# Statistics of the norms summed by TensorE, an opening with other DMA order, and ScalarE costs of the planner changed

## The chip, the cores and the metric

The kernel runs on one core of one Trainium2 chip. The metric is the device time of one execution in microseconds, the lower the better. TensorE (PE in the profile) multiplies, VectorE (DVE) and ScalarE (ACT) work element by element, GpSimd (POOL) computes a few powers, and SyncE (SP) issues most of the loads. Each engine works through its own instructions in the order in which the program wrote them.

## The reference, cut to what matters

Two layers act on 512 latent tokens and 256 context tokens of width 1024. Each layer is a modulated RMSNorm, one input projection, three parallel groups (a two-way mLSTM, a gated MLP over chunks, a convolution module), an output projection with a gated residual, then a second modulated RMSNorm, a SwiGLU of width 2816 and another gated residual. A last RMSNorm ends it. All of it is in float32.

```python
def rmsnorm(t, g):
    t32 = t.astype(jnp.float32)
    y = t32 * lax.rsqrt(jnp.mean(t32 * t32, axis=-1, keepdims=True) + EPS)
    return (y * g).astype(t.dtype)
...
px = (rmsnorm(x, norm1_g[l]) * (1.0 + sc1) + sh1) @ w_in[l] + b_in[l]
...
x = x + g1 * (y_x @ w_out[l])
x = x + g2 * swiglu(rmsnorm(x, norm2_g[l]) * (1.0 + sc2) + sh2, w_gu[l], w_down[l])
...
return rmsnorm(x, final_g)
```

The shifts `sh` and scales `sc` come from a product of the conditioning vectors with `w_mod`. The mean of the squares over the 1024 features of each token is the "statistic" of which this study speaks.

## The kernel before, in words

**Layout.** The residual stream `xT` lies with features on the partitions: 8 tiles (k = 0 to 7) of 128 features by 768 tokens. Tokens come in two groups, `GA` (the 512 latent ones) and `GB` (the 256 of the context); the second half of layer 1 splits the latent ones into `GX0` and `GX1` of 256 each. Every large product is done three times, with a high and a low part of each operand: high by high, high by low, low by high (lines 528, 529 and 530 in `tiles`). ACT makes the high part (a cast), DVE the low part (a subtraction): for weights `hi` and `lo` (lines 457 and 334, 374 and 376), for normalised activations the two halves of `HH` (lines 868 and 879). PE can start the second product of a step only when the low half of `HH` is there.

**A norm.** `square` has ACT square a tile of `xT` as soon as its residual is added, and DVE adds it to a running sum `acc` (line 781). With all 8 tiles in, `rstd_rows` has PE multiply each piece of 128 tokens of the sum with a column of 1/1024 (`stat`, line 831). DVE adds EPS (`ms`, line 837), POOL takes the power -0.5 (`rs`, line 264), PE spreads the result over the partitions (`rstdb`, line 846). Then for each k DVE makes the normalised tile `nt` (line 914), and ACT and DVE its two halves in `HH`. Only the last norm, `final`, leaves its last square out of the running sum: there PE multiplies the square tile too and accumulates in PSUM.

**The opening.** `start` clears constants, ACT's queue loads `cT` into `csil` (a tile with 32 columns per k, of which two are loaded), `ident`, and the small parameters `cv[0]`, then later `masks` and `cv[1]`; ACT applies SiLU to `csil` in place. SP's queue loads `xT` in four pieces of two k each, then the weights in the order that `ORDER` sets: quarters of `w_mod` (`modq`, products `modps` on PE at line 670, and `modT` at 687) between the first projection weights. `early_stats` squares all 768 tokens of each k on ACT (line 793), DVE adds them one after the other into one tile (line 800, seven additions), and PE makes the statistic of both groups from the sum (line 815, 6 instructions). A float32 matmul shows as two rows in the trace: 6 instructions are 12 passes.

**What sets the order.** Nothing is scheduled on the chip: while the program is built, a planner (`Plan`) runs all steps as coroutines. A step names an engine and an estimate of its duration, and the planner emits next what could start earliest by its estimates. So each estimate (`ACT(n)` is 95 + 0.833 n ns, `ACTP(n)` 190 + 0.833 n, `DVE2`, `STT`, `PE`, `MM` and so on) moves instructions on every engine, and on the chip each engine then keeps to that order. DMAs report on one of eight semaphores that are handed out in turn over all queues, in the order of emission. A DMA that is given a semaphore which is still in use waits on its queue until the earlier DMA has landed.

## Time and profile before

| | |
|---|---|
| median of 3 runs | 1536.78 us (1536.64 to 1539.75) |
| the profiled execution | 1534.92 us |
| its span, first to last instruction | 1533.1 us |
| granted TensorE clock, mean | 0.995 |
| PE busy | 1488.5 us |
| DVE busy | 1147.0 us |
| ACT busy | 686.0 us |
| POOL busy | 33.7 us |

The profiled execution takes 1.8 us more than its span and 1.86 us less than the median. A busy engine is one that has an instruction in flight. "Idle before" with a releaser is time in which the engine had nothing in flight, and what ended it.

### The profile page before, as it was taken

The page shows a single profiled execution, that of the slowest core. Times are in us where ns is not written, and L with a number is a line of the kernel's source. Part 1 is how long each engine was busy: PE and PEld are TensorE (multiplying, and loading weights), DVE is VectorE, ACT ScalarE, POOL GpSimd, SP SyncE. Part 2 cuts the span into 40 slices and gives each one's busy share as a digit, 9 for nine tenths or more (in the row PEclk, how much of TensorE's full clock was granted, in tenths as well). Part 3 has the DMA queues.
Part 4 walks back from the last instruction along what each step waited for, and adds up shares of the span by engine and source line. Part 5 has one row for each costly group of instructions (what it writes and reads, how often), then busy time and mean ns, then how long its engine had stood idle before and what let it go on. Part 6 is the DMA issues. An engine that isn't in the chain of part 4 may idle for free.

```text
span 1533.1 us, 26131 instructions
## 1 busy us (share of the span) xinstructions
PE 1488.5 (97%) x10212; PEld 1390.5 (91%) x10212; DVE 1147.0 (75%) x2430; ACT 686.0 (45%) x1428; POOL 33.7 (2%) x50
## 2 busy tenths in 40 slices
PE   5999999999999999999999999999999999999997
PEld 4887888888899999999999998778999999999997
DVE  5569988865898896777767773696767977877865
ACT  4332257644643343433333343416656554544534
POOL 0000010000000000000000000000100000000000
PEclk9999999999999999999999999999999999999999
DMA  9434244423143434343433332213332233333331
GB/s 327 171 125 133 69 140 146 128 83 120 60 138 104 145 97 151 97 124 124 128 120 124 111 98 76 76 60 102 103 111 70 83 103 105 104 97 100 105 98 64
DMA packets 73848, 173.25 MB, mean 113 GB/s; under 512 B 7564, under 2 KB 19964, under 8 KB 73724
## 3 DMA queue, kind: packets, MB, share of 16 engines
q1 hardware_dynamic: 70956, 170.16, 35.0%
q10 hardware_dynamic: 2768, 1.42, 0.3%
q8 instruction: 80, 1.31, 0.3%
q14 instruction: 44, 0.36, 0.1%
HBM read 169.34 MB, written 2.21 MB: 112 GB/s over the span
## 4 chain that ended last, share of the span: by engine, by line
PE 81%; DVE 11%; DMA 4%; ACT 2%; issue 2%; POOL 0%; SPq 0%; POOLq 0%; DVEq 0%; ACTq 0%
PE mm L528 14%; PE mm L529 14%; PE mm L530 14%; PE bA L1912 5%; PE bA L1913 5%; PE bA L1914 5%; PE bC L1912 2%; PE bC L1913 2%; PE bC L1914 2%; DVE lo L376 1%; DMA raw<-in_wgu 1%; DVE lo L334 1%; PE bB L1912 1%; PE vp L1325 1%; PE bB L1913 1%
## 5 line engine op out<-in xcount | busy, mean ns | idle before, releaser
L528 PE MATMUL mm<-HH,hi 128*128 128x256 f32 (+2 forms) x1040 | 349.3, 336 | 0.2 <-ACT HH L1624 0.2
L529 PE MATMUL mm<-HH,hi 128*128 128x256 f32 (+2 forms) x1040 | 337.5, 324 | 5.6 <-DVE HH L879 4.5
L530 PE MATMUL mm<-HH,lo 128*128 128x256 f32 (+2 forms) x1040 | 336.7, 324 | 0.6 <-DVE lo L334 0.6
L374 ACT CAST hi<-raw 128x512 fp32r<-128x512 f32 (+2 forms) x361 | 209.6, 599 | 240.2 <-PE mm L529 46.2
L376 DVE TENSOR_TENSOR lo<-raw,hi 128x512 fp32r<-128x512 f32 (+2 forms) x361 | 229.0, 659 | 28.6 <-ACT hi L374 25.5
L528 PEld LDWEIGHTS mm<-HH,hi 128*128 128x128 f32 x1040 | 196.5, 189 | 18.8 <-issue 6.4
L529 PEld LDWEIGHTS mm<-HH,hi 128*128 128x128 f32 x1040 | 196.8, 189 | 18.0 <-DVE HH L879 5.6
L530 PEld LDWEIGHTS mm<-HH,lo 128*128 128x128 f32 x1040 | 196.3, 189 | 15.8 <-DVE lo L334 0.8
L528 PE MATMUL mm<-ffn,hi 128*128 128x256 f32 (+1 forms) x544 | 167.4, 308 | 0.0
L529 PE MATMUL mm<-ffn,hi 128*128 128x256 f32 (+1 forms) x544 | 167.0, 307 | 0.0
L530 PE MATMUL mm<-ffn,lo 128*128 128x256 f32 (+1 forms) x544 | 166.7, 307 | 0.1
L2051 DVE SCALAR_TENSOR_TENSOR xT<-mm,modc,xT 128x256 f32<-128x256 f32 (+2 forms) x208 | 96.1, 480 | 77.7 <-PE mm L530 77.2
L457 ACT CAST hi<-raw 128x1024 fp32r<-128x1024 f32 (+4 forms) x92 | 87.8, 963 | 129.1 <-PE mm L529 61.5
L1913 PE MATMUL bA<-T,hi 128*128 128x384 f32 (+1 forms) x468 | 145.4, 311 | 0.0
L334 DVE TENSOR_TENSOR lo<-raw,hi 128x1024 fp32r<-128x1024 f32 (+4 forms) x92 | 102.2, 1119 | 54.1 <-ACT hi L457 49.6
L727 DVE SCALAR_TENSOR_TENSOR macc<-raw,csil,macc 128x512 f32<-128x512 f32 x168 | 122.3, 743 | 0.8
L420 DVE TENSOR_TENSOR raw<-raw 128x512 f32<-128x512 f32 x156 | 103.8, 686 | 23.6 <-DMA raw<-in_wgu 22.8
L1912 PE MATMUL bA<-HH,hi 128*128 128x256 f32 (+1 forms) x384 | 112.1, 292 | 0.5 <-ACT d L1986 0.5
L1914 PE MATMUL bA<-HH,lo 128*128 128x256 f32 (+1 forms) x384 | 111.9, 291 | 0.0
L528 PEld LDWEIGHTS mm<-ffn,hi 128*128 128x128 f32 x544 | 102.3, 188 | 0.8 <-issue 0.6
L530 PEld LDWEIGHTS mm<-ffn,lo 128*128 128x128 f32 x544 | 102.2, 188 | 0.4 <-DVE lo L376 0.4
L529 PEld LDWEIGHTS mm<-ffn,hi 128*128 128x128 f32 x544 | 102.3, 188 | 0.0
(273 smaller groups left out, 3016.5 us busy)
## 6 DMA issues: line engine op xcount, KB each, us to landing
raw<-in_wmod SPq DMA_DIRECT2D x96, 512.0 KB, 3.8
raw<-in_wgu SPq DMA_DIRECT2D x88, 512.0 KB, 3.6
raw<-in_wb SPq DMA_DIRECT2D x36, 512.0 KB, 3.6
pbt<-dr SPq DMA_DIRECT2D x40, 256.0 KB, 3.6
raw<-in_wd SPq DMA_DIRECT2D x40, 256.0 KB, 2.6
raw<-in_wout SPq DMA_DIRECT2D x16, 512.0 KB, 3.6
raw<-in_wd SPq DMA_DIRECT2D x16, 384.0 KB, 3.3
raw<-in_wd SPq DMA_DIRECT2D x16, 320.0 KB, 2.8
```

Of the source, the lines that this page charges most:

```text
L334: dve.tensor_tensor(lo, r, hi.bitcast(F32), ALU.subtract)
L374: act.copy(hi, x)
L376: dve.tensor_tensor(lo, x, hi.bitcast(F32), ALU.subtract)
L420: dve.tensor_tensor(o, x, y, op)
L528: pe.matmul(o, lhsT=hi[:, k, :], rhs=hh, start=(j == 0), stop=False)
L529: pe.matmul(o, lhsT=hi[:, k, :], rhs=hl, start=False, stop=False)
L530: pe.matmul(o, lhsT=lo[:, k, :], rhs=hh, start=False, stop=(j == nk - 1))
L727: dve.scalar_tensor_tensor(a[g], s[:, i, :], c, a[g], ALU.mult, ALU.add)
L1912: pe.matmul(o, lhsT=hi[:, k], rhs=rh, start=start and k == 0, stop=False, skip_group_check=True)
L1913: pe.matmul(o, lhsT=hi[:, k], rhs=rl, start=False, stop=False, skip_group_check=True)
L1914: pe.matmul(o, lhsT=lo[:, k], rhs=rh, start=False, stop=k == 3, skip_group_check=True)
L2051: dve.scalar_tensor_tensor(x, p[:, a - h["t0"]:b - h["t0"]], MODC[l][:, 5, d, g["g"]:g["g"] + 1], x, ALU.mult, ALU.add)
```

## The change

1. `early_square` and `early_stats`: DVE adds only the pairs of k 0 and 1, 2 and 3, 4 and 5 (three additions). PE multiplies each of the three pair sums, and the squares of k = 6 and of k = 7 as they are, with the column of 1/1024, all accumulated in PSUM: 5 times 6 instructions in place of 6.
2. `square`: in every norm, no longer in the last alone, the eighth square can go to PE by itself. DVE's eighth addition is left out, and PE has twice as many statistic instructions there. The condition is read when the eighth square is emitted and seven sums are done.
3. `start`: `cT` is loaded into a tile of its own, `cin`, contiguous on both sides, and SiLU writes from it into `csil`. `masks` and `cv[1]` move from ACT's queue to SP's, behind the first norm.
4. Seven activations are planned at `ACTP`, 95 ns more each, in place of `ACT`.

```diff
     def square(k, grp, then):
         n, t0 = grp["n"], grp["t0"]
-        if then is final and ACC.get(t0, (0, 0, 0))[2] == KD - 1:
+        if ACC.get(t0, (0, 0, 0))[2] == KD - 1:
             yield W(ACC[t0][1])
...
             ACC[t0].append(s)
-            yield from final(grp)
+            yield from then(grp)
             return
...
-        if k:
+        if k % 2 == 0 and k < 6:
+            odd[k + 1] = s
+            fire(ev("sq", k))
+            return
+        if k < 6:
             yield W(ev("sq", k - 1))
             yield DVE2(T)
-            dve.tensor_tensor(a[0], a[0], s, ALU.add)
+            dve.tensor_tensor(s, s, odd[k], ALU.add)
             release("slot")
-        fire(ev("sq", k))
+        if k > 1:
+            yield W(ev("st", k - 2 if k < 7 else 6))
+        for g, q in p:
+            for j in range(g["n"] // P):
+                yield MM(P)
+                pe.matmul(q[:, j:j + 1], lhsT=s[:, g["t0"] + j * P:g["t0"] + (j + 1) * P], rhs=onesD,
+                          start=(k == 1 and j == 0), stop=(k == KD - 1), skip_group_check=True)
...
     def norm_lo(tag, l, which, t, k, grp):
...
-        yield ACT(n)
+        yield ACTP(n)
         act.activation(h[:, 0, k, o:o + n], t, AF.Identity, bias=sh)
...
-        act.dma_start(out=csil[:, :, 0:2], in_=cT_d)
+        act.dma_start(out=cin, in_=cT_d)
...
-        act.activation(csil[:, :, 0:2], csil[:, :, 0:2], AF.Silu)
+        act.activation(csil[:, :, 0:2], cin, AF.Silu)
...
-        act.dma_start(out=masks, in_=mk_d)
-        act.dma_start(out=cv[1], in_=cv_d[1])
         spawn(early_stats(), 0.5)
+        yield W(ev("h", 0, 0, 0, KD - 1))
+        yield DMA(P * (256 + NCV) * 4)
+        sp.dma_start(out=masks, in_=mk_d)
+        sp.dma_start(out=cv[1], in_=cv_d[1])
```

The other `ACTP` edits are of the same form: `norm_copy`, and the evacuations of the conv gate, q, o and u columns.

What this does to the order is shown at three places. On SP's queue at the start, before (`DMAHW0` to `DMAHW7` are the eight semaphores, and "waits" is what the DMA waits for ahead of its issue):

```order
L308 DMA xT_69<-in_xT 128x1536 x3
L308 DMA xT_69<-in_xT 128x1536 [waits DMAHW0_49]
L328 DMA raw_112<-in_wmod 128x4x256 [waits DMAHW1_49]
L328 DMA raw_129<-in_wmod 128x4x256 [waits DMAHW2_49]
L328 DMA raw_135<-in_wb 128x1024 [waits DMAHW3_49]
```

The same place after:

```order
L309 DMA xT_69<-in_xT 128x1536 x4
L329 DMA raw_113<-in_wmod 128x4x256
L329 DMA raw_130<-in_wmod 128x4x256 [waits DMAHW0_49]
L329 DMA raw_136<-in_wb 128x1024 [waits DMAHW1_49]
L329 DMA raw_147<-in_wmod 128x4x256 [waits DMAHW2_49]
```

`DMAHW0` is that of the load of `cT` in both. Before, the fourth piece of `xT` waits for it; after, the second load of `w_mod` does, and four pieces of `xT` and one load of `w_mod` wait for nothing.

On PE at the start, before (`stat` is the statistic, `modps` and `modT` the modulation, `rstdb` the spread of the reciprocal root, `mm` the first projection):

```order
L670 MATMUL modps<-raw,csil 32x128 x16
L687 MATMUL modT<-sel_79,mq 128x4
L815 MATMUL stat<-onesD,sq 128x1 x6
L670 MATMUL modps<-raw,csil 32x128 x16
L846 MATMUL rstdb<-ident,rs 128x128 x2
L687 MATMUL modT<-sel_79,mq 128x4
L846 MATMUL rstdb<-ident,rs 128x128 x4
L670 MATMUL modps<-raw,csil 32x128 x8
L528 MATMUL mm<-HH,hi 128x256
```

And after:

```order
L810 MATMUL stat<-onesD,sq 128x1 x12
L671 MATMUL modps<-raw,csil 32x128 x8
L810 MATMUL stat<-onesD,sq 128x1 x6
L671 MATMUL modps<-raw,csil 32x128 x8
L810 MATMUL stat<-onesD,sq 128x1 x6
L688 MATMUL modT<-sel_80,mq 128x4
L810 MATMUL stat<-onesD,sq 128x1 x6
L671 MATMUL modps<-raw,csil 32x128 x16
L854 MATMUL rstdb<-ident,rs 128x128 x2
L688 MATMUL modT<-sel_80,mq 128x4
L854 MATMUL rstdb<-ident,rs 128x128 x4
L671 MATMUL modps<-raw,csil 32x128 x16
```

The statistic stands in five groups of 6 instructions, the first two ahead of all modulation and the others between its loads; one more load of modulation (8 instructions) stands ahead of the first `mm`.

On DVE where layer 1 begins, from the `ms` of GB on, before (`xT` is a residual addition, `lo` the low part of a weight, `kb` a small scaling, `HH` the low half of the normalised tile):

```order
L781 TENSOR_TENSOR acc<-acc,sq 128x512
L2051 SCALAR_TENSOR_TENSOR xT<-mm,modc_82,xT 128x384
L914 SCALAR_TENSOR_TENSOR nt<-xT,gs,rstdb 128x256
L334 TENSOR_TENSOR lo<-raw,hi 128x1024
L1689 TENSOR_SCALAR kb<-cv_81 128x4
L914 SCALAR_TENSOR_TENSOR nt<-xT,gs,rstdb 128x256
L781 TENSOR_TENSOR acc<-acc,sq 128x512
L2051 SCALAR_TENSOR_TENSOR xT<-mm,modc_82,xT 128x384
L334 TENSOR_TENSOR lo<-raw,hi 128x1024
L879 SCALAR_TENSOR_TENSOR HH<-nt,modc_83,HH 128x256
L914 SCALAR_TENSOR_TENSOR nt<-xT,gs,rstdb 128x256
L879 SCALAR_TENSOR_TENSOR HH<-nt,modc_83,HH 128x256
```

And after:

```order
L922 SCALAR_TENSOR_TENSOR nt<-xT,gs,rstdb 128x256
L2059 SCALAR_TENSOR_TENSOR xT<-mm,modc_83,xT 128x384
L922 SCALAR_TENSOR_TENSOR nt<-xT,gs,rstdb 128x256
L335 TENSOR_TENSOR lo<-raw,hi 128x1024
L1697 TENSOR_SCALAR kb<-cv_82 128x4
L922 SCALAR_TENSOR_TENSOR nt<-xT,gs,rstdb 128x256
L887 SCALAR_TENSOR_TENSOR HH<-nt,modc_84,HH 128x256
L2059 SCALAR_TENSOR_TENSOR xT<-mm,modc_83,xT 128x384
L335 TENSOR_TENSOR lo<-raw,hi 128x1024
L782 TENSOR_TENSOR acc<-acc,sq 128x512
L887 SCALAR_TENSOR_TENSOR HH<-nt,modc_84,HH 128x256
L922 SCALAR_TENSOR_TENSOR nt<-xT,gs,rstdb 128x256
```

The first `HH` of the context group has moved ahead of one `lo` and one `acc`; the second now stands behind an `xT`, a `lo` and an `acc` that follow the first. In the same stretch PE has `stat` with 4 instructions in place of 2 for GB; for GA it keeps 4, since there the eighth square is emitted before the seventh sum is done, so the condition of the change does not hold. In the other five between the opening and `final` it holds: 12 more instructions in all (2 for GB and 4 for GA in the second norm of layer 0, 2 for GB here, 2 each for GX0 and GX1 in the second norm of layer 1). The order of the last stretch, the final norm, is the same as before.

More of the change, by code (lines that the diff above doesn't have):

```diff
@@ L253, in backbone @@
     csil = pers.tile([P, KD, 32], F32, name="csil")
+    cin = pers.tile([P, KD, 2], F32, name="cin")
     ex8 = pers.tile([P, 8], F32, name="ex8")
@@ L787, in backbone, with early_square @@
     RB = {}
-    def early_square(k, a):
+    def early_square(k, p, odd):
         yield A("slot")
@@ L793, in early_square @@
         act.activation(s, xT[:, k, :], AF.Square)
-        if k:
+        if k % 2 == 0 and k < 6:
[3 more added lines that the diff above has]
+        if k < 6:
             yield W(ev("sq", k - 1))
-        else:
-            a.append(s)
-        if k:
             yield DVE2(T)
-            dve.tensor_tensor(a[0], a[0], s, ALU.add)
+            dve.tensor_tensor(s, s, odd[k], ALU.add)
             release("slot")
-        fire(ev("sq", k))
+        if k > 1:
[5 more added lines that the diff above has]
+                          start=(k == 1 and j == 0), stop=(k == KD - 1), skip_group_check=True)
+        release("slot")
+        fire(ev("st", k))
+        if k == 5:
+            fire(ev("st", 4))
     def early_stats():
-        acc = []
+        yield A("ps", 2)
+        p, odd = [(g, ps("stat")) for g in (GB, GA)], {}
         for k in range(KD):
             yield W(ev("x", k - k % 2))
-            spawn(early_square(k, acc), 0.4)
-        yield W(ev("sq", KD - 1))
-        for g in (GB, GA):
-            yield A("ps")
-            p = ps("stat")
-            for j in range(g["n"] // P):
-                yield PE(P)
-                pe.matmul(p[:, j:j + 1], lhsT=acc[0][:, g["t0"] + j * P:g["t0"] + (j + 1) * P], rhs=onesD, start=True, stop=True)
-            spawn(norm(0, 0, g, p[:, 0:g["n"] // P]), 0.4 if g is GB else 0.5)
-        release("slot")
+            spawn(early_square(k, p, odd), 0.4)
+        yield W(ev("st", KD - 1))
+        for g, q in p:
+            spawn(norm(0, 0, g, q[:, 0:g["n"] // P]), 0.4 if g is GB else 0.5)
     def rstd_rows(grp, p=None):
@@ L889, in norm_copy @@
         yield W(ev(l, "ffnmem"))
-        yield ACT(n)
+        yield ACTP(n)
         act.activation(FORM[l, k % 4][:, k // 4, t0:t0 + n], t, AF.Identity, bias=sh)
@@ L1226, in evac @@
                 t0, n = grp["t0"], grp["n"]
-                yield ACT(n, "sigmoid")
+                yield ACTP(n, "sigmoid")
                 act.activation(st["cacc"][:, c, t0:t0 + n], p, AF.Sigmoid, bias=col(l, CV_BG + c))
@@ L1389, in evac @@
                 t0, n = grp["t0"], grp["n"]
-                yield ACT(n)
+                yield ACTP(n)
                 act.activation(q_[h][:, t0:t0 + n], p, AF.Identity, bias=col(l, CV_BQ + h))
@@ L1399, in evac @@
                 t0, n = grp["t0"], grp["n"]
-                yield ACT(n)
+                yield ACTP(n)
                 act.activation(st["og", h // 2][:, h % 2, t0:t0 + n], p, AF.Identity, bias=col(l, CV_BO + h))
@@ L1418, in evac @@
                 t0, n = grp["t0"], grp["n"]
-                yield ACT(n)
+                yield ACTP(n)
                 act.activation(st["u", 0][:, c, t0:t0 + n], p, AF.Identity, bias=col(l, CV_BU + c))
```

## The prediction

> **What bounds the kernel now.** I read the page first, then who waited for whom on PE, then the opening and the start of layer 1 in order of time.
>
> ```profile
> span 1533.1 us, 26131 instructions
> ...
> PE 1488.5 (97%) x10212; PEld 1390.5 (91%) x10212; DVE 1147.0 (75%) x2430; ACT 686.0 (45%) x1428; POOL 33.7 (2%) x50
> ...
> PE   5999999999999999999999999999999999999997
> ```
>
> PE is the bound: 1488.5 of 1533.1 us, and in slices of 38 us only the first and the last are not full. So whatever PE is given more to do costs its own duration, and only an idle stretch of PE can be won back: 44.6 us in all. PE's waits over the whole span, sum, number and longest:
>
> ```profile
> PE modps L670 <- DMA raw<-in_wmod: 16.7, 2, 16.4
> PE mm L529 <- DVE HH L879: 4.5, 4, 2.6
> ...
> PE bA L1912 <- ACT x L1986: 1.1, 2, 0.8
> ```
>
> More than a third is the 16.4 us ahead of the first matmul. The next largest is the wait of a first product of a norm for the low half of its activations. The opening in order of time, and SP's own longest wait there:
>
> ```profile
> 0.74 9.13 SPq L308 DMA_DIRECT2D xT<-in_xT  x4
> 9.54 0.22 ACT L2168 ACTIVATE csil<-csil 128x16 f32<-128x16 f32 x1 [5.39 <-DMA csil<-in_cT]
> 9.91 0.98 SPq L328 DMA_DIRECT2D raw<-in_wmod  x2
> 10.44 5.97 ACT L793 ACTIVATE sq<-xT 128x768 f32<-128x768 f32 x8 [0.68 <-issue]
> 12.05 7.34 DVE L800 TENSOR_TENSOR sq<-sq 128x768 f32<-128x768 f32 x7 [1.99 <-ACT sq L793]
> 16.38 1.08 PE L670 MATMUL modps<-raw,csil 128*32 128x128 f32 x16 [16.38 <-DMA raw<-in_wmod]
> 19.25 0.59 PE L687 MATMUL modT<-sel,mq 128*128 128x4 f32 x2 [0.38 <-ACT mq L682]
> 19.70 2.70 PE L815 MATMUL stat<-onesD,sq 128*128 128x1 f32 x12
> 22.32 1.93 PE L670 MATMUL modps<-raw,csil 128*32 128x128 f32 x32
> 24.19 1.22 PE L846 MATMUL rstdb<-ident,rs 128*128 128x128 f32 x4
> 27.28 0.65 PE L670 MATMUL modps<-raw,csil 128*32 128x128 f32 x16
> 27.86 0.38 PE L528 MATMUL mm<-HH,hi 128*128 128x256 f32 x1
> ```
>
> ```profile
> SPq L308 <- DMA csil<-in_cT: 7.4, 1, 7.4
> ```
>
> ```profile
> 8.00:12.00 4.00, 0.00 (x0) 0.00 (x0) 0.33 (x2) 1.77 (x4) 0.00 (x0) 1.00 0.63 145
> 12.00:20.00 8.00, 2.92 (x36) 2.01 (x36) 6.83 (x8) 5.49 (x9) 0.00 (x0) 1.00 1.05 369
> ```
>
> The fourth piece of `xT` waits 7.4 us for the tiny load of `cT`, and everything behind it on SP's queue with it. From 8 to 12 us the DMA engines move 145 GB/s (last column) where they move 369 right after. That hole is what part 3 of the change fills.
>
> **The opening, step by step.** The loads that matter, KB each and median us to landing, from the answer on DMAs up to 45 us:
>
> ```profile
> xT<-in_xT SPq DMA_DIRECT2D x4, 768.0 KB, 6.1
> ...
> cv<-in_cv ACTq DMA_DIRECT2D x2, 81.0 KB, 7.8
> masks<-in_mk ACTq DMA_DIRECT2D x1, 128.0 KB, 5.1
> ```
>
> Without the wait, the loads come earlier. The hole is worth (369 - 145) / 369 x 4 = 2.4 us of transfer, and `masks` and `cv[1]` (128 and 81 KB) another 0.6 us at that rate, so about 3.0 us: the first `w_mod` lands near 13.4 in place of 16.4. SP's queue meets the two moved loads only behind the first norm, ahead of weights not yet due; I cost that at nothing, at worst the 0.6 us.
>
> The statistic starts earlier still. A piece of `xT` lands 6.1 us after its issue at the median, so the second, issued a little after 0.74, near 7.3; the first needs 768 KB less at 369 GB/s, 2.1 us, so I estimate it at 5.2. Two squares (5.97 / 8 = 0.75 each) and one addition (7.34 / 7 = 1.05) end near 7.8. Then PE takes over, and here is the price. One group of 6 instructions is 12 passes; from the start of `stat` at 19.70 to the next row at 22.32 that took 2.62 us. Five groups are 13.1 us of PE, where DVE saves four additions that nothing will wait for any more. Along PE's new order: two groups to 13.0; the first modulation load (lands 13.4; 0.93, half of 22.32 to 24.19) to 14.3; a group to 16.9; a load to 17.9; a group to 20.5; `modT` (19.25 to 19.70) to 20.9; the last group to 23.5. Before, the statistic ended at 22.32. So `rstdb` comes 1.2 us later, although all data are there earlier: the wait for DMA has become PE's own queue.
>
> Of the 24 added instructions, those up to 13 us are hidden under time in which PE was idle anyway; the last three groups are not. Behind `rstdb` one more load of modulation (27.28 to 27.86, 0.58) stands ahead of the first `mm`; that is work moved, not added. Opening: **+1.2 us**. Bounds: -3.0 if the statistic keeps ahead of the loads, +2.7 if the half clock lasts through the first products as well (1.5 more, half of the 3 us to the end of `modps` and `mm` behind `rstdb`).
>
> **At which clock?** The 2.62 us hold only at the clock of that row. Later in the program the same work is quicker:
>
> ```profile
> 369.48 0.50 PE L831 MATMUL stat<-onesD,acc 128*128 128x1 f32 x4
> 384.36 1.05 PE L831 MATMUL stat<-onesD,acc 128*128 128x1 f32 x8
> 915.75 1.70 PE L831 MATMUL stat<-onesD,acc 128*128 128x1 f32 x8
> ```
>
> ```profile
> 911.10:914.50 3.40, 0.78 (x7) 0.77 (x6) 3.40 (x7) 2.17 (x4) 0.00 (x0) 1.00 0.35 92
> 914.50:917.90 3.40, 3.40 (x18) 3.38 (x17) 2.48 (x7) 1.13 (x3) 0.10 (x1) 0.50 0.43 145
> 917.90:921.30 3.40, 3.40 (x18) 3.40 (x18) 2.18 (x6) 1.53 (x3) 0.91 (x1) 0.50 0.01 2
> 921.30:924.70 3.40, 3.40 (x31) 3.40 (x31) 2.30 (x4) 1.19 (x2) 0.00 (x0) 1.00 0.00 0
> ```
>
> Eight passes take 1.05 us at full clock and 1.70 at 0.50 (the column behind the POOL figure). The opening's 12 in 2.70 are 0.225 each, like 1.70 / 8 = 0.21 and not like 1.05 / 8 = 0.13: the opening's statistic ran at half clock, though its clock is not recorded. Would 13 us of statistic lift it? From 914.5 to 917.9 PE was never idle, 1.7 of its 3.4 us were statistic, and the clock stayed at 0.50; it rose only after 3.4 us of products alone. In the opening PE ran from 19.25 on nearly without a pause, and the clock was still low at 24.19 (four passes of `rstdb` in 1.22 us). Both say that passes of one column do not raise the clock, so I take half clock.
>
> The Trainium skill, TensorE: Matmul & The Clock Gate, Part 1: The HAM clock gate, speaks for the other side: it says that about 3.4 us of sustained activity release full clock. By that rule the statistic would lift its own clock after its second group, and the sum would be that of the first rival. The stretch from 914.5 to 917.9 disagrees, unless the rule means matrix columns and not occupied time.
>
> **The later norms.** Part 2 adds 12 instructions, 24 passes. At full clock one more pass costs (1.05 - 0.25) / 7 = 0.114 us, with 0.25 for a single one:
>
> ```profile
> L831 PE MATMUL stat<-onesD,acc x40: 164/250/352, 369.5 to 1524.5; 128*128 128x1 f32 x40
> ```
>
> So 2.7 us of PE. Half of it falls in layer 0's second norm, where PE has no idle time to hide it (140 us with 139.98 busy):
>
> ```profile
> 300.00:440.00 140.00, 139.98 (x846) 121.23 (x845) 100.33 (x177) 71.08 (x124) 1.71 (x2) 1.00 0.33 103
> ```
>
> There DVE's saved additions are off the path: **+1.4 us**. The other half is in layer 1, where PE does wait for the norm:
>
> ```profile
> 904.86 0.43 DVE L781 TENSOR_TENSOR acc<-acc,sq 128x256 f32<-128x256 f32 x1 [0.54 <-ACT sq L778]
> 912.07 1.21 DVE L334 TENSOR_TENSOR lo<-raw,hi 128x1024 fp32r<-128x1024 f32 x1
> 913.20 0.47 DVE L879 SCALAR_TENSOR_TENSOR HH<-nt,modc,HH 128x256 fp32r<-128x256 f32 x1
> 913.73 0.38 PE L529 MATMUL mm<-HH,hi 128*128 128x256 f32 x1 [2.62 <-DVE HH L879]
> 913.99 0.48 DVE L879 SCALAR_TENSOR_TENSOR HH<-nt,modc,HH 128x256 fp32r<-128x256 f32 x1
> ```
>
> In each such norm an addition of 0.43 leaves the chain and four passes of 0.114 = 0.46 enter it: nothing won or lost. What the order does matters more. The first low half of GB loses an addition and a `lo` (1.21) ahead of it, but takes a normalisation more (0.48) and meets the later `nt`: I lay it out 0.8 earlier, near 912.85. The second one stands behind an `xT`, a `lo` and an addition (0.61 + 1.21 + 0.69) and ends near 915.8 in place of 914.5. PE's one wait of 2.62 becomes two, about 1.5 and 2.2, and some of the second is made good because 12 products stand ahead of GA's statistic in place of 8. I take **+0.6** (from -2 to +3). In the second norm of layer 1 three low halves come together: PE's first wait grows and its second goes; I take 0.
>
> **The seven ACTP costs** move rows within the mixing stages by a few places. Behind the opening the most that PE waits for any one line of ACT is the 1.1 us of the third row of waits above, so a better order has little to win; I take **-0.5** (-2 to +2).
>
> Sum: 1.2 + 1.4 + 0.6 + 0 - 0.5 = **+2.7 us**. On the profiled execution that is 1534.92 + 2.7 = 1537.6; the median of the runs shown is 1.86 higher, so 1536.78 + 2.7 = **1539.5**. A measurement of this kernel can tell about 0.2%, 3.1 us, from no change.
>
> **Rivals.**
> 1. The statistic does lift the clock. For it: PE is occupied without a pause from 7.8 on. Against: the two stretches above. Then a group is 12 x 0.114 = 1.4 us after the second, PE waits for the loads again, and these are 3.0 us earlier: -3.0 + 1.4 + 0.6 - 0.5 = -1.5, some 1535.3, with up to 1.5 more where PE was itself behind its loads.
> 2. The half clock at 914.5 is gone. It cost half of 6.8 us, 3.4. For it: the idle stretch of 2.62 is cut in two, and it was 2.62 in the 3.4 us up to 914.5 that brought it. Against: the two new stretches sum to more. Then 2.7 - 3.4 = -0.7, 1536.1. The Trainium skill, TensorE: Matmul & The Clock Gate, Part 1: The HAM clock gate, says that one idle window of about 3.4 us halves the clock. In this trace 2.62 us idle and 0.78 busy did.
> 3. Slower: the second low half of GB decides. If PE waits more than about 2.2 us for it at 915.8, a second period at half clock is opened behind the first, while GA's statistic, also at half clock, pushes the rest of the norm: 2.7 + 3.4 = +6.1, 1542.9. For it: the order of DVE shown. Against: PE arrives there with other work still in hand if my layout of DVE is late by a microsecond.
> 4. The change does less than it says: GA in layer 1 keeps its old sum. That is in the order, and counted.
>
> **How the numbers follow.** Forecast 0.42, rival 1 0.23, rival 2 0.12, rival 3 0.15, other 0.08. The forecast's case runs about 2 us either way, so 0.25 of it is within 0.2% and 0.17 above 1539.85. Rival 1 gives 0.09 faster, 0.13 same, 0.01 slower; rival 2 gives 0.03, 0.08, 0.01; rival 3 0.02 same, 0.13 slower; the rest 0.03, 0.01, 0.04. Sums: faster 0.15, same 0.49, slower 0.36. The range reaches from rival 1 with a further gain, 1532.5, to just above rival 3, 1543.5.
>
> **What would show it.** Right: `stat` in the opening at about 0.21 us a pass and ending near 23.5; `rstdb` between 24.5 and 26; the fourth `xT` issued by 2.2 us; 24 passes more at L839. Wrong: passes of 0.11 in the opening, `rstdb` before 22 (rival 1); a granted clock of 1.00 around 915 (rival 2); a half clock of over 7 us there (rival 3).

## The result, and the profile after

The changed kernel takes 1546.88 us (median of four, 1545.35 to 1549.15) beside 1538.26 for the kernel before in the same comparison (1536.64 to 1540.54). The ratio is 1.0053, with a 95% interval of 1.0032 to 1.0073: slower by 4.9 to 11.2 us. The prediction said 1539.5 and at most 1543.5. It was wrong.

The profiled execution took 1545.85 us. First its page, the span and PE's row:

```profile
span 1544.1 us, 26260 instructions
...
PE 1505.4 (97%) x10284; PEld 1411.4 (91%) x10284; DVE 1139.6 (74%) x2421; ACT 686.1 (44%) x1428; POOL 34.5 (2%) x50
```

PE is busy for 16.9 us more (1488.5 before) and idle for 5.9 less (38.7 in place of 44.6). Most of the 5.9 is its earlier start, at 11.15 in place of 16.38. So waits did not get longer: PE worked longer. The 72 rows added are those forecast, 48 in the opening and 24 in the later norms; at 0.114 us each they would be 8.2 us.

The opening in order of time, and last two rows from the start of layer 1 (start, duration, engine, line, out<-in, count, and in brackets the idle time before and its end):

```profile
5.93 1.56 ACT L795 ACTIVATE sq<-xT 128x768 f32<-128x768 f32 x2
...
7.95 0.17 DVE L2180 TENSOR_TENSOR sel<-ident 128x4 f32<-128x4 f32 x1 [6.46 <-DMA ident<-in_id]
...
10.07 0.17 DVE L1697 TENSOR_SCALAR kb<-cv 128x4 f32<-128x4 f32 x1 [1.95 <-DMA cv<-in_cv]
10.15 2.69 DVE L803 TENSOR_TENSOR sq<-sq 128x768 f32<-128x768 f32 x3
...
11.15 5.28 PE L810 MATMUL stat<-onesD,sq 128*128 128x1 f32 x24 [11.15 <-DVE sq L803]
...
16.36 1.08 PE L671 MATMUL modps<-raw,csil 128*32 128x128 f32 x16
...
17.37 2.72 PE L810 MATMUL stat<-onesD,sq 128*128 128x1 f32 x12
...
24.04 2.70 PE L810 MATMUL stat<-onesD,sq 128*128 128x1 f32 x12
...
26.67 1.93 PE L671 MATMUL modps<-raw,csil 128*32 128x128 f32 x32
...
28.53 1.22 PE L854 MATMUL rstdb<-ident,rs 128*128 128x128 f32 x4
...
29.82 1.14 PE L854 MATMUL rstdb<-ident,rs 128*128 128x128 f32 x8
...
32.30 0.39 PE L529 MATMUL mm<-HH,hi 128*128 128x256 f32 x1 [0.33 <-ACT HH L876]
...
33.68 0.39 PE L530 MATMUL mm<-HH,hi 128*128 128x256 f32 x1 [1.00 <-DVE HH L887]
...
36.13 0.50 PE L530 MATMUL mm<-HH,hi 128*128 128x512 f32 x1 [0.53 <-DVE HH L887]
...
922.65 0.38 PE L530 MATMUL mm<-HH,hi 128*128 128x256 f32 x1 [0.87 <-DVE HH L887]
...
925.30 0.39 PE L530 MATMUL mm<-HH,hi 128*128 128x256 f32 x1 [1.68 <-DVE HH L887]
```

The squares of the first pair are done at 7.5, but DVE's first addition starts only at 10.15. It stands in DVE's queue behind `sel`, which waits for `ident`, and behind `kb`, which waits until 10.07 for the parameters in `cv`. So the statistic starts at 11.15, and from there to 29.8 PE has no gap. All the same its passes take 0.22 each up to 26.7, and `rstdb` takes 0.31 a pass at 28.53 and 0.14 at 29.82: PE was occupied for over 18 us on end before its clock rose. (The durations have to tell this: up to 29.8 the view's column for the clock reads 1.00, since the trace holds no record of it before the first change.) `rstdb` comes 4.3 us later than before (24.19), the first product 4.4 later (27.86).

Next, windows of the clock's own grid (columns: window; length, then busy time and rows of PE, PEld, DVE, ACT and POOL; the granted clock; share and GB/s of the DMA engines). In every trace the changes of the clock lie on a grid of 3.413 us, whose phase differs from run to run. Two after the opening, then the start of layer 1:

```profile
33.22:36.64 3.42, 2.27 (x23) 1.46 (x23) 3.42 (x9) 2.11 (x4) 0.00 (x0) 1.00 1.10 349
36.64:40.05 3.41, 3.41 (x25) 2.47 (x24) 0.25 (x1) 0.27 (x1) 0.00 (x0) 0.50 1.06 385
...
115.14:118.56 3.42, 1.93 (x17) 0.93 (x17) 3.14 (x14) 1.03 (x1) 0.00 (x0) 1.00 0.76 258
118.56:121.97 3.41, 3.41 (x17) 3.41 (x17) 3.20 (x12) 1.29 (x2) 0.00 (x0) 0.50 0.10 42
...
920.69:924.10 3.41, 2.06 (x13) 1.59 (x11) 3.41 (x6) 2.46 (x5) 0.00 (x0) 1.00 0.27 82
924.10:927.51 3.41, 2.21 (x18) 2.18 (x18) 3.41 (x9) 1.59 (x3) 0.00 (x0) 1.00 0.46 154
927.51:930.93 3.42, 3.42 (x17) 3.42 (x17) 2.83 (x8) 1.59 (x4) 1.01 (x1) 0.50 0.03 7
```

The window with waits of the first products behind the opening (1.15 us idle in it, on `HH`) is followed by 3.4 us at half clock, and so is a window near 117 in which PE is busy for 1.93 us. At the start of layer 1 PE's one wait became two, the last two rows of the opening's view: 0.87 and 1.68, together 2.55 as against 2.62. The half clock behind them lasts 3.4 in place of 6.8 us.

These three differences can't be charged to the change. Of the eight traces below whose opening is that of the kernel before (its own included), five have a stretch at half clock near 33 and six one near 115; of the two other traces with the change's whole opening, neither has either. And the changed kernel without its new tile, with the same order on PE, has 6.8 us at half clock at the start of layer 1. Where the grid falls decides it.

### The profile page after: what moved, and what is told of

Read it like the earlier page. It is cut to its first block, busy times and chain, and to the rows that moved or that the text cites. A ratio compares the mean times of both kernels' runs of the same rounds, so it can differ in the third digit from the quotient of the medians.

```text
span 1544.1 us, 26260 instructions
## 1 busy us (share of the span) xinstructions
PE 1505.4 (97%) x10284; PEld 1411.4 (91%) x10284; DVE 1139.6 (74%) x2421; ACT 686.1 (44%) x1428; POOL 34.5 (2%) x50
## 4 chain that ended last, share of the span: by engine, by line
PE 84%; DVE 9%; DMA 3%; ACT 1%; issue 1%; POOL 0%; SPq 0%; ACTq 0%; POOLq 0%; DVEq 0%
PE mm L529 15%; PE mm L530 14%; PE mm L531 14%; PE bA L1920 5%; PE bA L1921 5%; PE bA L1922 5%; PE bC L1920 3%; PE bC L1921 3%; PE bC L1922 3%; DVE lo L335 1%; PE bB L1920 1%; PE bB L1921 1%; PE bB L1922 1%; PE vp L1333 1%; PE vp L1334 1%
## 5 line engine op out<-in xcount | busy, mean ns | idle before, releaser
L529 PEld LDWEIGHTS mm<-HH,hi 128*128 128x128 f32 x1040 | 199.0, 191 | 19.2 <-issue 6.4
L530 PEld LDWEIGHTS mm<-HH,hi 128*128 128x128 f32 x1040 | 199.4, 192 | 17.7 <-DVE HH L887 5.9
```

Of the source, the lines that this page charges most:

```text
L529: pe.matmul(o, lhsT=hi[:, k, :], rhs=hh, start=(j == 0), stop=False)
L530: pe.matmul(o, lhsT=hi[:, k, :], rhs=hl, start=False, stop=False)
```

## The experiments

Ratios are to the kernel before, run beside each on the same chip, with 95% intervals; 0.001 is 1.5 us.

### The parts one by one

**The opening alone.** The kernel before with the change's `early_square`, `early_stats`, `start` and `cin`:

```diff
-            dve.tensor_tensor(a[0], a[0], s, ALU.add)
+            dve.tensor_tensor(s, s, odd[k], ALU.add)
...
-        act.dma_start(out=csil[:, :, 0:2], in_=cT_d)
+        act.dma_start(out=cin, in_=cT_d)
```

> The kernel before with the opening of the change alone (its loads, its statistic); later norms and ACT's costs as before. Theory: the opening carries most of the loss. DVE's pair additions stand behind kb, which waits for cv's landing near 10.07, so the statistic starts at 11.1 in place of my 7.8, and its 13.4 us of passes then stand one behind the other on PE; rstdb comes near 28.5 and the first product near 32.3, as in the changed kernel, and the run is 5 to 6 us slower than before. Rival: the opening is made good further on (shorter waits in the mixing stage) and the loss comes from the later norms and their order: rstdb as late, but the run only 1 to 2 us slower.

1.0036 (1.0025 to 1.0047): 5.5 us slower. The opening carries most of the loss. The product that starts at 57.84 us before starts at 61.63, 3.8 later.

**The later norms alone.**

```diff
-        if then is final and ACC.get(t0, (0, 0, 0))[2] == KD - 1:
+        if ACC.get(t0, (0, 0, 0))[2] == KD - 1:
...
-            yield from final(grp)
+            yield from then(grp)
```

> The kernel before with the last square of every later norm on PE, nothing else. Theory: it costs its 24 passes less what the shorter wait at the start of layer 1 gives back: +1 to +3 us. Rival: it costs the greater part of the loss, +5 us or more, by new waits or half-clock stretches. Third: it wins, since the half clock at the start of layer 1 is cut from 6.8 to 3.4 us: -1 us.

1.0015 (1.0002 to 1.0027): 2.3 us slower, as its theory had it (my terms were 1.4 + 0.6). But the windows in layer 0's second norm show another sort of cost:

```profile
382.91:386.32 3.41, 3.20 (x29) 3.12 (x28) 1.89 (x3) 1.62 (x3) 0.00 (x0) 1.00 0.65 172
386.32:389.73 3.41, 3.41 (x19) 2.38 (x20) 0.17 (x1) 0.00 (x0) 1.01 (x1) 0.50 0.49 145
```

PE is busy for 3.20 of 3.41 us, and the clock halves all the same. 2.00 of the 3.20 are one-column statistic passes (from 384.10). The changed kernel's own profile has the same sixteen passes from 389.70 on, and its clock stays at 1.00 there (windows from 388.21 to 395.04), so such passes don't bring the stretch on in every run. This window raised the question of the next group.

**ACT's costs alone.** The seven `ACTP` in place of `ACT`:

```diff
-        yield ACT(n)
+        yield ACTP(n)
         act.activation(h[:, 0, k, o:o + n], t, AF.Identity, bias=sh)
```

> The kernel before with the measured costs of ACT's evacuations alone. Theory: no difference that shows, within 1.5 us either way. Rival: the new order adds waits or a half-clock stretch behind 30 us: 3 us or more slower.

0.9993 (0.9980 to 1.0006): no difference that shows, as forecast.

**The loads alone**, with DVE's sum as before:

```diff
-        act.dma_start(out=csil[:, :, 0:2], in_=cT_d)
+        act.dma_start(out=cin, in_=cT_d)
...
-        act.dma_start(out=masks, in_=mk_d)
+        sp.dma_start(out=masks, in_=mk_d)
```

> The kernel before with the change's loads alone (cT in a tile of its own, masks and the second cv behind the first norm); the squares are summed by seven additions on DVE and six instructions on PE, as before. Theory: the loads bring what I counted, and only the statistic on PE ate it. The additions start behind kb near 10.2 and end 7.3 later, near 17.6; the statistic ends near 20.3, rstdb comes near 22.2 in place of 24.19, and the run is 2 us faster (1 to 3). Rival: the opening is bound by the chain of the norm, not by loads: rstdb at 24 and no difference. The change's loads are harmful in themselves (the moved masks): slower by 1 us or more.

```profile
10.20 7.33 DVE L801 TENSOR_TENSOR sq<-sq 128x768 f32<-128x768 f32 x7
...
22.10 1.22 PE L847 MATMUL rstdb<-ident,rs 128*128 128x128 f32 x4
```

`rstdb` comes 2.1 us earlier, as expected. The whole run does not show it: 0.9992 (0.9980 to 1.0004). What took it back was open at this point; the last group of experiments has a cause that is large enough.

**The statistic alone**, with the loads as before:

```diff
         if k:
-            yield DVE2(T)
-            dve.tensor_tensor(a[0], a[0], s, ALU.add)
+        for g, q in p:
+            for j in range(g["n"] // P):
+                pe.matmul(q[:, j:j + 1], lhsT=s[...], rhs=onesD, ...)
```

> The kernel before with the change's statistic in the opening alone (three pair additions, five groups on PE); the loads as before. With the runs on the opening and on the loads alone this completes the square of the two. Theory: the squares end at 11.9 at the earliest, the first pair addition near 12.9; 13.4 us of narrow passes at half clock, two loads and modT stand behind it on PE, so rstdb comes near 30, 6 later than before, and the run is 6 to 7 us slower: the statistic is the loss, and the loads take 1 to 2 of it back. Rival: without the early loads the passes lie under the wait for them, which lasts to 16.4 here: rstdb near 27, 3 us slower.

```profile
13.48 5.28 PE L809 MATMUL stat<-onesD,sq 128*128 128x1 f32 x24 [13.48 <-DVE sq L802]
...
30.86 1.22 PE L853 MATMUL rstdb<-ident,rs 128*128 128x128 f32 x4
```

`rstdb` 6.7 us later, about as expected (6) and not covered by the wait for loads; the run 1.0027 (1.0015 to 1.0039), 4.2 us slower where 6 to 7 were expected. In the opening the statistic is the loss. The earlier loads bring `rstdb` forward as much with it (2.3 us, 30.86 to 28.53) as without it (2.1).

### Why the statistic is so late and so dear

**The late start.** The changed kernel with one more wait ahead of `kb`:

```diff
             yield W(ev("cv"))
+            yield W(ev("st", 5))
             yield DVE1(4)
             dve.tensor_scalar(st["kb"], cv[l][:, CV_BK:CV_BK + H], float(P) ** -0.5, None, ALU.mult)
```

> The changed kernel with kb moved behind DVE's three pair additions, nothing else. Theory: the late start is DVE's queue behind cv's landing at 10.07; now the first addition follows sel (7.95) at 8.1, the statistic starts near 8.7 (what I had forecast at 7.8), and as PE has nothing but its own queue, rstdb comes near 26.2 in place of 28.5: 2 us faster than the changed kernel, still 6 slower than the kernel before. Rival: PE is bound by the loads of modulation, not by the start: the statistic starts earlier, rstdb stays at 28.5, no difference to the changed kernel.

```profile
8.13 0.95 DVE L803 TENSOR_TENSOR sq<-sq 128x768 f32<-128x768 f32 x1
9.14 5.28 PE L810 MATMUL stat<-onesD,sq 128*128 128x1 f32 x24 [9.14 <-DVE sq L803]
...
26.52 1.22 PE L854 MATMUL rstdb<-ident,rs 128*128 128x128 f32 x4
```

The start is 2.0 us earlier and `rstdb` is 2.0 earlier, one for one: PE is bound by its own queue, and `kb` was 2.0 of the 3.35 us by which I had the start too early. The run is at 1.0043 (1.0027 to 1.0058), still slower; that it gains on the changed kernel (1.0053) is seen in the trace alone, since the two intervals overlap.

**The same with DVE's sum.** The run with the loads alone, `kb` behind the seven additions:

```diff
             yield W(ev("cv"))
+            yield W(ev("sq", KD - 1))
```

> The kernel with the change's loads alone, and kb behind the seven additions of DVE. Theory: the additions start at 8.1 and are held only by ACT's squares, the last of which ends near 13.3; they end near 15.5, the statistic near 18.2, rstdb comes near 20.1 (24.19 in the kernel before, 22.10 with the loads alone), and the run is 4 us faster than the kernel before, but for new stretches at half clock. Rival: loads 3 and 4 of the modulation (landing near 17.3 and 18.8) hold PE: rstdb near 21 and at most 3 us. Second rival: the half clock takes it back elsewhere, as in the profile of the kernel with the loads alone: rstdb near 20, the run within 1 us of the kernel before.

```profile
7.77 7.33 DVE L801 TENSOR_TENSOR sq<-sq 128x768 f32<-128x768 f32 x7
...
20.65 1.22 PE L847 MATMUL rstdb<-ident,rs 128*128 128x128 f32 x4
```

`rstdb` 3.5 us earlier than before. Yet the run is at 1.0000 (0.9988 to 1.0013).

**Does a one-column pass count as work?** The kernel before; in layer 0's second norm each statistic matmul is preceded by seven copies whose result is not used:

```diff
+                    for _ in range(7 if len(REP) < 2 else 0):
+                        pe.matmul(p[:, 256:257], lhsT=s[:, i * P:(i + 1) * P], rhs=onesD, start=True, stop=True)
```

> The kernel before; in the second norm of layer 0 each statistic instruction is preceded by seven idle copies of itself into unused columns, so that GA's statistic is 64 one-column passes with PE never idle. Theory: one-column passes count as idle for the clock; with 7.3 us of them (0.114 each) at least one window of 3.4 us holds nothing else, and the granted clock falls to 0.50 near 385, though PE waits for nothing. Rival: the clock follows PE's occupied time, as I took it in my second rival; it stays at 1.00 and the run is 84 x 0.114 = 9.6 us slower and no more.

And once more with 128 columns in each copy:

```diff
+                        pe.matmul(p[:, 256:256 + P], lhsT=s[:, i * P:(i + 1) * P], rhs=ident, start=True, stop=True)
```

> As the run with the narrow copies, but the seven copies have 128 columns (the identity in place of the column of ones), with the same weights loaded. Theory: the clock stays at 1.00 through the second norm of layer 0, and the added time is that of the passes alone. Rival: it falls here too, so the width is not what counts.

The windows with narrow copies:

```profile
392.66:396.07 3.41, 3.41 (x33) 3.41 (x32) 0.00 (x0) 0.00 (x0) 0.00 (x0) 1.00 0.71 280
396.07:399.48 3.41, 3.41 (x18) 3.41 (x18) 0.00 (x0) 0.00 (x0) 0.00 (x0) 0.50 0.00 0
399.48:402.90 3.42, 3.42 (x17) 3.42 (x17) 0.16 (x1) 0.00 (x0) 1.01 (x1) 0.50 0.00 0
```

With wide ones:

```profile
391.66:395.07 3.41, 3.41 (x30) 3.41 (x31) 0.00 (x0) 0.00 (x0) 0.00 (x0) 1.00 0.89 293
395.07:398.49 3.42, 3.42 (x33) 3.42 (x33) 0.00 (x0) 0.00 (x0) 0.00 (x0) 1.00 0.04 14
398.49:401.90 3.41, 3.41 (x33) 3.41 (x32) 0.36 (x2) 0.00 (x0) 1.01 (x1) 1.00 0.02 5
```

In both PE is busy without a pause. The narrow passes halve the clock after one window, the wide ones never. And a row of each shows that the width costs next to nothing, 14 passes at full clock:

```profile
391.64 1.72 PE L832 MATMUL stat<-onesD,acc 128*128 128x1 f32 x14
```

```profile
391.65 1.83 PE L832 MATMUL stat<-ident,acc 128*128 128x128 f32 x14
```

The theory holds: here the granted clock follows the width of what PE streams, not the time for which it is occupied. The copies differ in their values too (ones against the identity); the next run, with the same ones in 128 columns, leaves that rival out. Each kernel ran once, in 1551.53 and 1548.70 us, so these times carry no interval.

**The changed kernel with a wide statistic.** The column of ones is broadcast to 128 columns, and one result column is read:

```diff
-                pe.matmul(q[:, j:j + 1], lhsT=s[...], rhs=onesD,
+                pe.matmul(q[:, j * P:(j + 1) * P], lhsT=s[...], rhs=onesD.to_broadcast([P, P]),
...
-                    pe.matmul(p[:, i:i + 1], lhsT=s[...], rhs=onesD, ...)
+                    pe.matmul(p[:, i * P:(i + 1) * P], lhsT=s[...], rhs=onesD.to_broadcast([P, P]), ...)
```

> The changed kernel, with every statistic matmul 128 columns wide (the column of ones broadcast, one of the 128 equal result columns read), same order and number of instructions. Theory: the statistic's narrow passes kept PE at half clock from 11 to 29.8 although it never waited; wide passes cost the same 0.12 at full clock and count as work, so the clock rises after one or two windows, near 15 to 18; the later groups take 1.4 in place of 2.7, rstdb comes near 23 to 24 in place of 28.5, and the run is 4 to 6 us faster than the changed kernel, within 1.5 of the kernel before. Rival: the width changes nothing in the opening (the clock rises with the first products only): rstdb at 28.5, 8 us slower than the kernel before.

```profile
11.28 4.31 PE L810 MATMUL stat<-onesD,sq 128*128 128x128 f32 x24 [11.28 <-DVE sq L803]
...
16.09 1.60 PE L810 MATMUL stat<-onesD,sq 128*128 128x128 f32 x12
...
22.31 0.71 PE L855 MATMUL rstdb<-ident,rs 128*128 128x128 f32 x4
```

A group takes 1.60 in place of 2.72, `rstdb` comes at 22.31 in place of 28.53, and the run is at 1.0004 (0.9995 to 1.0013). With no instruction moved, added or taken away, the changed kernel falls from 1.0053 to no difference from the kernel before. Full clock in the statistic makes good nearly the whole loss, the late start included: `rstdb` is now 1.9 earlier than before the change (24.19).

**The later norms with a wide statistic.** The run with the later norms alone, and

```diff
-                    pe.matmul(p[:, i:i + 1], lhsT=s[...], rhs=onesD, ...)
+                    pe.matmul(p[:, i * P:(i + 1) * P], lhsT=s[...], rhs=onesD.to_broadcast([P, P]), ...)
```

> The kernel before with the last square of the later norms on PE, as in the run with that part alone, and these statistic matmuls 128 columns wide. Theory: part of the 2.3 us that this part cost is the half clock which 16 narrow passes brought on near 386; wide, that stretch is gone and 0.5 to 1.5 us remain. Rival: the cost is the passes and the order alone: again 2 to 3 us.

1.0006 (0.9995 to 1.0017), 0.9 us; the trace has no half clock in layer 0's second norm or at the start of layer 1. The two intervals, of 2.3 and 0.9 us, overlap, so the gain is not settled; and since the changed kernel has no stretch in that norm with narrow passes either, one trace without it doesn't settle that the width took it away here.

### Filling the waits

**A warm PE in the opening**, on the run with the loads and `kb` behind; the idle matmuls multiply broadcast constants and nothing reads them; the opening's statistic is wide too:

```diff
+            pe.matmul(WARM[0][:, 0:P], lhsT=onesD.to_broadcast([P, P]), rhs=onesD.to_broadcast([P, P]), start=True, stop=True)
...
+        warmup(34)
...
+                    warmup((3, 2)[len(WARM) - 1])
```

> The kernel with the change's loads and kb behind the additions, with 34 idle 128-column matmuls ahead of PE's first load and 3 and 2 behind the first two loads, and the opening's statistic wide. Theory: the clock is up before 12.9, so the statistic takes 1.4 in place of 2.7 and every load 0.5 in place of 0.94; rstdb comes near 19.3 in place of 20.65, the first product near 22.5 in place of 24.55, and the run is 2 us faster than with cold PE. Rival: PE stands behind DVE's additions and the loads in either case, rstdb stays at 20.5; no difference. The idle matmuls end late: the first load starts behind 13.5 and the run is slower.

```profile
20.46 0.71 PE L858 MATMUL rstdb<-ident,rs 128*128 128x128 f32 x4
...
24.11 0.91 PE L677 MATMUL modps<-raw,csil 128*32 128x128 f32 x16 [1.79 <-DMA raw<-in_wmod]
```

0.9986 (0.9975 to 0.9996): faster, the first version that is. But not by the way expected: `rstdb` comes at 20.46, hardly sooner than with cold PE (20.65), and the first product at 24.95, not sooner. PE now waits for the fifth load of modulation, so the opening is bound by loads; in the trace the clock still fell twice there. The interval overlaps that of the run with cold PE (0.9988 to 1.0013), so that the idle matmuls themselves win anything is not shown.

**The changed kernel with all mends** (`kb` behind, wide statistic, 22 idle matmuls):

```diff
+        warmup(22)
```

> The changed kernel with all three mends: kb behind the pair additions, the statistic wide everywhere, 22 idle 128-column matmuls ahead of the statistic. Theory: at full clock a group takes 1.4, PE waits for the loads again, the last group ends near 18.6 and rstdb comes near 20.4 in place of 28.53: 8 us faster than the changed kernel, 1 to 3 faster than the kernel before. It is what the change would have been by my first rival. Rival: the later norms and new half-clock stretches take it back: within 1 us of the kernel before.

0.9991 (0.9980 to 1.0002). `rstdb` comes at 20.38, as worked out: the changed statistic costs nothing any more once its clock is up, and wins nothing over DVE's sum.

**The wait at the start of layer 1**, in the kernel before:

```diff
+        if (l, which, k, t0) == (1, 0, 0, NX):
+            for _ in range(10):
+                pe.matmul(FILL[t0][:, 256:256 + P], lhsT=onesD.to_broadcast([P, P]), rhs=onesD.to_broadcast([P, P]), start=True, stop=True)
         fire(ev("h", l, which, t0, k))
```

> The kernel before with ten idle 128-column matmuls (2.4 us at 0.12 a pass) ahead of the first product of layer 1, where PE waits 2.62 us for the norm. Theory: what the wait costs beyond itself is the half clock that follows; filled, the clock stays at 1.00 from 911 on, and half of 6.8 us, 3.4, is won. Rival: GA's narrow statistic and the rest of the waiting in the next window still halve it for one window or more: 1.7 us or nothing. The idle matmuls wait for DVE's reads of the tile they write and come too late: nothing won, or 1 us lost.

```profile
914.40:917.80 3.40, 3.33 (x27) 3.01 (x25) 3.40 (x7) 2.01 (x3) 0.00 (x0) 1.00 0.32 91
917.80:921.20 3.40, 3.36 (x27) 3.11 (x27) 3.40 (x10) 1.53 (x3) 0.04 (x1) 1.00 0.41 154
```

No half clock is left there, and the run is at 0.9983 (0.9972 to 0.9994): 2.6 us faster by ten multiplications that nobody needs. DVE's work had set the wait, so nothing came late: the second product starts 3.06 us after the last one of the stage ahead (915.01 to 918.07), as before (910.66 to 913.73). The time was won from the half clock behind the wait. That isn't chance of the grid: of the 17 traces without these products all but one have 3.4 to 10.2 us at half clock there, and none of the three with them.

### Where the rest went

In every profile with the change's tile for `cT`, the feed-forward stage of layer 1 ran at a slower pace than without it, though PE waits for next to nothing between the stage's ends. Between the rows shown below, and among the kernels with the old later norms, it takes 301.84 to 302.38 us in the seven profiles without a new tile and 303.26 to 304.01 in the six with one, the next run's among them.

**Sixty-four bytes.** The kernel before, with a tile of that size in the same place and never read:

```diff
+    pad = pers.tile([P, KD, 2], F32, name="pad")
...
+        dve.memset(pad, 0.0)
```

> The kernel before with one more persistent tile of 64 bytes a partition, where the change puts cT's own tile, set to zero once and never read: every later tile lies 64 bytes further on. In all profiled runs with the change's tile for cT the feed-forward stage of layer 1 (1195 to 1485 us of the kernel before) took 1.0 to 2.0 us longer, with nothing reordered there and no more waits; in those without it, 0.4 longer at most. Theory: the tile's 64 bytes do it, by where the operands of PE lie: the stretch takes 1 to 2 us longer here too and the run is 1 to 2 slower. Rival: it comes from the moved loads or from run to run: the stretch within 0.4 of the kernel before.

The two ends of the stage before:

```profile
1174.01 0.39 PE L529 MATMUL mm<-HH,hi 128*128 128x256 f32 x1 [1.03 <-DVE HH L879]
...
1475.88 0.38 PE L1912 MATMUL bA<-HH,hi 128*128 128x256 f32 x1 [0.46 <-ACT d L1986]
```

And with the tile:

```profile
1180.59 0.39 PE L530 MATMUL mm<-HH,hi 128*128 128x256 f32 x1 [1.01 <-DVE HH L880]
...
1484.45 0.39 PE L1913 MATMUL bA<-HH,hi 128*128 128x256 f32 x1 [0.46 <-ACT d L1987]
```

301.87 us became 303.86, with the same instructions on PE in the same order. The run is at 1.0016 (1.0003 to 1.0029), 2.5 us slower for a tile that does nothing.

**The best version, with all that helped**: the loads, `kb` behind DVE's sum, a wide statistic in all norms, idle matmuls in the opening and ahead of layer 1.

```diff
+        warmup(34)
...
+                    pe.matmul(p[:, i * P:(i + 1) * P], lhsT=s[...], rhs=onesD.to_broadcast([P, P]), ...)
...
+            for _ in range(10):
+                pe.matmul(FILL[t0][:, 256:256 + P], ...)
```

> All that helped together: the change's loads, kb behind the additions, DVE's sum, the statistic wide in all norms, idle matmuls in the opening and ahead of the first product of layer 1. Theory: the gains add: 2.2 of the opening (as measured), 3 of layer 1, some 5 us below the kernel before (1.5 to 7). Rival: new half-clock stretches of the mixing stage, which come with the phase of the clock's windows, hide it: within 2 us.

0.9960 (0.9946 to 0.9974): 6 us faster, where the runs with the warm opening (2.2) and the filled wait (2.6) together give 4.8. Within the interval the gains add.

**The best version without a new tile**, `cT` going into a part of layer 1's modulation tile that is written later:

```diff
-    cin = pers.tile([P, KD, 2], F32, name="cin")
...
+    cin = MODC[1][:, 0]
```

> The best version so far, with cT loaded into a part of layer 1's modulation tile that is written only later, so that no tile is added. Theory of the 64 bytes: the stretch of layer 1 is 1.8 us shorter and the run 7 to 8 us below the kernel before, in place of 6. Rival: as the best version.

0.9945 (0.9930 to 0.9961), 1529.45 us: 8.5 us faster than the kernel before, and the fastest here. The stage takes 302.38 us (1171.06 to 1473.44), with the tile 304.01. The intervals of the two runs overlap, so the tile's part is seen in the stage and not yet in the whole.

**The changed kernel without a new tile**, with the same two lines:

> The changed kernel with cT loaded into that same part of layer 1's modulation tile, no tile added. Theory of the 64 bytes: 1 to 2 us faster than the changed kernel, some 6 slower than the kernel before. Rival: no difference to the changed kernel.

The stage in the changed kernel, from a row that stands first in both:

```profile
1181.00 0.39 PE L530 MATMUL mm<-HH,hi 128*128 128x256 f32 x1 [0.63 <-DVE HH L887]
...
1487.27 0.38 PE L1920 MATMUL bA<-HH,hi 128*128 128x256 f32 x1 [0.46 <-ACT d L1994]
```

And without the tile:

```profile
1179.61 0.39 PE L530 MATMUL mm<-HH,hi 128*128 128x256 f32 x1 [0.67 <-DVE HH L887]
...
1483.54 0.39 PE L1920 MATMUL bA<-HH,hi 128*128 128x256 f32 x1 [0.46 <-ACT d L1994]
```

306.27 against 303.93 us, with one wait of 0.4 near 1183 in both. The run is at 1.0023 (1.0011 to 1.0035), 3.5 us slower than the kernel before where the change as given was 4.9 to 11.2. So the tile makes some 2 to 4 us of the loss. It is also enough to explain the two runs with the loads alone, within their intervals: what the earlier loads win in the opening, their tile takes back. No run had these loads alone without the tile. And the tile is not all of the stage's pace: the run with the later norms alone, with no new tile and the same order on PE in the stage, takes 302.85 (1178.50 to 1481.35). The further 1.1 us is not explained.

## Why the prediction was wrong

The sum was +2.7, and the runs of the parts give 5.5 + 2.3 - 1.1 = +6.7, with +8.1 (4.9 to 11.2) for the whole.

| term | forecast | measured |
|---|---|---|
| opening, with its tile | +1.2 (-3.0 to +2.7) | +5.5 (3.8 to 7.2) |
| of that, 64 bytes of tile | none | some +2.5 (0.5 to 4.5) |
| later norms | +1.4 + 0.6 + 0 | +2.3 (0.3 to 4.2) |
| ACT's costs | -0.5 (-2 to +2) | -1.1 (-3.1 to +0.9) |

1. **The step that failed first** is that two squares and one addition "end near 7.8. Then PE takes over". I had durations for squares and additions, but did not look at what stands ahead of the additions on DVE's queue: `sel` and `kb`, which wait for loads that land at 7.95 and 10.07. The start was 11.15. From there the chain runs as I laid it out (five groups of 2.7, loads between them), so it ends 3.2 later, 26.7 in place of 23.5. The run with `kb` moved gives 2.0 of it back. With these 3.2 and the tile's 2.3 (point 6) the sum of +2.7 would have been +8.2. That it meets the measured 8.1 so closely is luck, given the interval.
2. **The loads' gain** was sized rightly: 3.0 us forecast for the first load of modulation, whose product starts at 13.22 in the run with the loads alone in place of 16.38; at `rstdb` 2.1 of it are left, and 3.5 with `kb` behind. That PE's own queue eats it was right too.
3. **Half clock in the opening**: right as the forecast, and right against the first rival. When the clock rises depends on the grid: the last eight passes of `rstdb` took 1.14 us here, and 2.06 (from 30.03) in the changed kernel without the tile. I had the price of a pass, but not that the passes in the later norms can bring the half clock on as well.
4. **Later norms**: the term was right in size (2.0 forecast, 2.3 measured) but I had its make-up wrong. At the start of layer 1 the two waits of about 1.5 and 2.2 were 0.87 and 1.68; the half clock behind them was 3.4 us in the profile after and 6.8 in the run with that part alone, so what the waits were worth stays open. In layer 0's second norm I priced 12 passes at 1.4; the profile with that part alone had a half clock of 3.4 us besides, the one of the whole change had none.
5. **The third rival** had the right sign and, at 1542.9, lay nearest to the measured time, but its mechanism isn't borne out: the half clock at the start of layer 1 got no longer in the profile after. The stretches at 36.6 and 118.6, of which it doesn't speak, come with the grid and stand in runs with the old opening too.
6. **What no term covered** is the tile, 2.3 us in the stage (306.27 to 303.93). I costed part 3 by its transfers alone. It adds 64 bytes to a partition, and that moves every later tile.

The Trainium skill, TensorE: Matmul & The Clock Gate, Part 1: The HAM clock gate, says that sustained matmul activity releases the full clock after a window of about 3.4 us. With a wide statistic the run agrees (0.13 us a pass in the group at 16.09, 4.8 us after the start), with a narrow one it doesn't (over 18 us without a pause, mostly one-column passes): activity means columns here. The stretch from 914.5 to 917.9, on which the prediction rested its doubt, was read rightly.

## What to carry to other kernels

Before a chain is laid out from durations, read on each engine's queue what stands ahead of its first instruction, and which load that waits for. A matmul with few columns should be made wide if the result allows it, and a wait of PE that can't be removed may be filled with idle products: in both the gain is the clock of what follows, and only a run of the whole kernel tells whether it reaches the end. A small new tile is not free until the pace of the long stages has been compared.

## What the runs showed of the hardware

- In the 20 traces, from the first record of the clock on, a window of 3.413 us at full clock in which PE spent at most half of the time on anything but one-column statistic passes was followed by half clock every time, and one with 67% or more never; between the two it goes both ways. An idle window is not needed: 2.27 busy of 3.42 us was enough ahead of 36.6. Since the grid's phase differs from run to run, equal code meets half clock in one run and not in the next (the eight traces with the old opening); how much of the scatter of the times this makes is not shown.
- A float32 pass of 128 columns takes 0.13 us at full clock where one of a single column takes 0.12 (1.83 and 1.72 us for 14), each with weights of its own.
- PE's pace in the feed-forward stage of layer 1 differs by 0.7% (301.87 and 303.86 us) with tiles moved by 64 bytes. That the address does it is inferred from the tile being all that differs; what of the address decides is not known. No other shift was tried, and the stage of layer 0 didn't show it in the padded kernel (0.1 us at most in two stretches of 70 us and more).
